# Layer 1's windowed attention in program order on three engines, with its modulation row made in layer 0's FFN

## The chip, the core and the metric

The kernel runs on one core of a Trainium2 chip, as one program. A core has a matrix engine (TensorE, here PE, with its weight loads as PEld), VectorE (DVE), ScalarE (ACT) and GpSimd (POOL), and queues of transfers, most of which SyncE (SP) issues. The engines run side by side; each works through its own list of instructions in order and waits on semaphores for the others. The metric is the device time of one execution in microseconds (us): before, 2740.77 us in the median of three runs (2738.22 to 2741.01).

## What is computed

512 tokens of width 1024 and 256 context rows go through two transformer layers, and the tokens then through a third block. Every normalization is followed by a shift and a scale, and every branch by a gate; these rows come from `silu(c) @ w_mod[l] + b_mod[l]`, six of 1024 per layer. In layer 1 the mixer is windowed attention, in which 16 query heads share 4 key heads of 64:

```
h  = modulate(x, g_pre_mix[1], sh_m, sc_m)
q, k, v = split(h @ wo_in)             # 1024 + 256 + 256 columns; context: k, v alone
q, k = axial_rope(q), axial_rope(k)
one block of 128 queries:              # lax.map over 4 blocks
  s = [q.k(band of 3 blocks, |q-k| <= 128)/8, q.k(256 context)/8, sink[head]]
  p = softmax(s);  o = p[band] @ v + p[ctx] @ v_ctx
y = concat(o) @ wo_out
x = x + gt_m * rmsnorm(y, g_post_mix[1])
h = modulate(x, g_pre_ffn[1], sh_f, sc_f)
x = x + gt_f * rmsnorm(swiglu(h), g_post_ffn[1])
```

Both blocks of queries at an edge have two key blocks in the band, the inner ones three. All is float32; most matrix products are split into a high and a low part (three products for one).

## The kernel before

**Around the change.** Layer 0's FFN (`ffn_pair`, layer 0's tokens and context together) runs eleven iterations over pairs of hidden columns, and ends each with `mod_tick(ticks)`. A tick makes one half of a modulation row: it takes loaded weights of 1 MB each (`w_mod`) and adds them up, scaled per partition, by scalar_tensor_tensor on DVE (line 395). The halves stand in a list of what is to be made (`bg`), of which the FFN may take those it is allowed; what is left is taken by later callers of `mod_tick`, `unit_end` of layer 1's attention among them (two ticks after every second unit). Rows that are made long before their use are stored in DRAM (`parked`) and loaded again where they are used.

**Layer 1** (`layer1`) makes keys and values, then the queries in two halves of 512 columns. `odd_q(1)` makes the second half: matmuls for four token tiles, and behind each tile a rope on DVE and a turn (`stack_q`), which splits the tile into a high part (ACT, line 383) and a low part (DVE, line 386), transposes both on PE (line 407, two rows of x4) and copies them out. The turns go through a list `later`; the last ones are popped one by one while the attention runs.

**The attention** (`attention4`) has 16 units: 2 halves of heads x 4 query blocks x 2, with four heads in each. Units 0, 1, 6 to 9, 14 and 15 have four key tiles (scores 512 wide), the others five (640 wide). It is a generator, one step per key tile:
- `score`: matmuls into a pair of PSUM banks (`pr`, two pairs take turns; line 380, masks line 1436), the reduction to the row maximum (DVE, line 1441), a small operation (398), the exponential with its sum (ACT, line 389). For the second head of a pair: the sink's difference on DVE (392), its exponential on ACT (389, 128x2), an add (392) and a reciprocal (1459) on DVE, and on POOL the scaling of both heads (1462).
- `trans`: four transposes on PE (407) and a copy out on ACT (1469).
- `pv`: the products of a unit with the values (PE, line 1484), then the high part (ACT, 383 into hTh) and the low part (DVE, 386 into hTl) of the result.

Scores run six heads ahead of the transposes. The loop spreads a unit's four scores over its key tiles (with five tiles none before the first), each followed by its `trans`, and calls `pv` of the unit before behind the second. After every score `self.stream.pump(1)` may issue one step of the weight stream: a load, or the split of a loaded weight (ACT line 263, DVE line 264; 1024 wide).

**What sets the order.** A scheduler orders each engine's instructions. Inside `with self.in_order(...)` the engines named keep the order in which the code emits them. For the attention PE alone is named: DVE and ACT are ordered by the scheduler there. Four steps of the generator run before `odd_q(1)`, and the others behind it, each followed by one turn out of `later`.

Of the kernel before, what the change touches and what calls it, by code (L numbers as in the profile page):

```python
# [339 lines left out]
class Core:  # L340
# [1078 lines left out]
    def attention4(self, units, v, odst, unit_end, ahead=6):  # L1419
        nc = self.nc  # L1420

        def score(u, h):
            n, c1, g = u["n"], u["col0"], h // 2
            if h == 0:
                u["sm"], u["nm"] = [self.small(2) for _ in range(2)], [self.small(2) for _ in range(2)]
                u["p"] = []
            sm, nm = u["sm"][g], u["nm"][g]
            sp = self.pair()
            q = u["q"][h]()
            for c0, k, w in u["pieces"][g]:  # L1430
                out = sp.ap[:, c0:c0 + w]
                ms = [m for m in u["mask"] if c0 <= m[0] < c0 + w]
                self.mm(out, q, k(0), start=True)
                self.mm(out, q, k(1), stop=not ms)
                for i, (mc, mi) in enumerate(ms):
                    nc.tensor.matmul(sp.ap[:, mc:mc + P], self.identb, self.maskb[:, mi * P:mi * P + P],
                                     start=False, stop=i == len(ms) - 1, skip_group_check=True)
            s = sp.ap[:, c1:c1 + n]
            i = h % 2
            m = nm[:, i:i + 1]  # L1440
            nc.vector.reduce_max(m, s, axis=AX.X)  # L1441
            if u["sink"] is None:
                self.t1(m, m, u["nscale"][h], ALU.mult)
            else:
                at = u["sink"][g]
                self.ts(m, m, -0.125, self.nsink[:, at + i:at + i + 1], ALU.mult, ALU.min)
            p = self.page()
            self.act(p.ap[:, 0:n], s, AF.Exp, scale=u["scale"][h], bias=m, accum_out=sm[:, i:i + 1])
            sp.done()
            u["p"].append(p)  # L1450
            if i == 0:
                return
            r = self.small(2)
            if u["sink"] is not None:
                es = self.small(2)
                self.tt(es, nm, self.nsink[:, at:at + 2], ALU.subtract)
                self.act(es, es, AF.Exp)
                self.tt(sm, sm, es, ALU.add)
            nc.vector.reciprocal(r, sm)
            for i in range(2):  # L1460
                p = u["p"][2 * g + i].ap[:, 0:n]
                nc.gpsimd.tensor_scalar(p, p, r[:, i:i + 1], 0.0, op0=ALU.mult, op1=ALU.add)  # L1462

        def trans(u, kt):
            b = self.bank()
            for h in range(4):
                self.tr(b.ap[:, P * h:P * h + P], u["p"][h].ap[:, kt * P:kt * P + P])
            pt = self.slot()
            nc.scalar.copy(pt.ap, b.ap)  # L1469
            b.done()  # L1470
            if kt == len(u["kt"]) - 1:
                for p in u["p"]:
                    p.done()
            return pt

        def pv(u, pts):

            ob = self.bank()
            last = len(pts) - 1
            for kt, pt in enumerate(pts):  # L1480
                vv = v(u["kt"][kt], u["kvs"])
                for g in range(2):
                    r = 64 * g
                    nc.tensor.matmul(ob.ap[r:r + 64, 0:256], vv[:, r:r + 64], pt.ap[:, 256 * g:256 * g + 256],  # L1484
                                     start=kt == 0, stop=kt == last, skip_group_check=True)
                pt.done()
            src = ob.ap[:, 0:256].rearrange("p (k n) -> p k n", k=2)
            dh, dl = odst(u, 0), odst(u, 1)
            self.hi(dh, src)
            self.lo(dl, src, dh)  # L1490
            ob.done()
            unit_end(u)

        self.psum.layout(True)
        waiting = deque((u, h) for u in units for h in range(4))
        for _ in range(ahead):
            score(*waiting.popleft())
            yield
        prev = None
        for u in units:  # L1500
            n, pts = len(u["kt"]), []
            for kt in range(n):
                for _ in range(4 * (kt + 1) // n - 4 * kt // n):
                    if waiting:
                        score(*waiting.popleft())
                        self.stream.pump(1)
                pts.append(trans(u, kt))
                yield
                if kt == 1 and prev:
                    pv(*prev)  # L1510
            prev = u, pts
        pv(*prev)
        self.psum.layout(False)
        yield

# [157 lines left out]
    def ffn_pair(self, win, wout, l, vecs, mid, ticks):  # L1673
# [56 lines left out]
        for j in range(11):  # L1730
            eg = st.need(("fm", win, l, 0, 8, 256 * j))
            eu = st.need(("fm", win, l, 0, 8, HID + 256 * j))
            at = [(eg, 0), (eg, 1), (eu, 0), (eu, 1)]
            bx, bc = [], []
            if j == 0:
                subs = [st.get(*a) for a in at]
                bx = [self.bank() for _ in range(4)]
                for h in range(2):
                    for i, s in enumerate(subs):
                        self.fm(bx[i].ap[:, H * h:H * h + H], s, 0, acts, range(8), H * h, H)  # L1740
                        if h == 1 and mid and i == 1:
                            mid.popleft()()
                while mid:
                    mid.popleft()()
            for i in range(4):
                if i % 2 == 0:
                    bc.append(self.bank())
                s = subs[i] if j == 0 else st.get(*at[i])
                if j:
                    bx.append(self.bank())  # L1750
                    self.fm(bx[i].ap, s, 0, acts, range(8), 0, TOK)
                self.fm(bc[i // 2].ap[:, CTX * (i % 2):CTX * (i % 2) + CTX], s, 0, acts, range(8), TOK, CTX)
                s.done()
            if j == 10:
                strict = self.in_order(mybir.EngineType.Activation, mybir.EngineType.DVE)
                strict.__enter__()
            hx.append(self.page())
            if j % 2 == 0:
                hc.append(self.page())
            for i in range(2):  # L1760
                g = self.slot()
                self.act(g.ap, bx[i].ap, AF.Silu)
                self.tt(hx[j].ap[:, TOK * i:TOK * i + TOK], g.ap, bx[2 + i].ap, ALU.mult)
                bx[i].done()
                bx[2 + i].done()
                g.done()
            g, o = self.slot(), 512 * (j % 2)
            self.act(g.ap, bc[0].ap, AF.Silu)
            self.tt(hc[j // 2].ap[:, o:o + 512], g.ap, bc[1].ap, ALU.mult)
            for b in bc + [g]:  # L1770
                b.done()
            self.mod_tick(ticks)
            if j == 9:
                hidden.prep(0)
                hidden.prep(1)
# [16 lines left out]
    def layer1(self):  # L1792
# [6 lines left out]
        later = deque(self.carry)  # L1799
# [68 lines left out]
        def odst(u, i):  # L1868
            a = 4 * u["kvs"] + 2 * u["hp"]
            return self.hT[i][:, a:a + 2, u["o"] * P:u["o"] * P + P]  # L1870

        def unit_end(u):
            if u["hp"] == 1:
                qT.pop((u["o"], u["kvs"])).done()
                self.mod_tick(2)
        attn = self.attention4(units, v, odst, unit_end)
        for _ in range(4):
            next(attn)
        later = self.odd_q(1)
        self.rope_b.done()  # L1880
        with self.in_order(mybir.EngineType.PE):
            for _ in attn:
                if later:
                    later.popleft()()
        for b in kT + kcp + [V, Vc]:
            b.done()
# [498 lines left out]
```

## Time and profile before

| | before |
|---|---|
| median of 3 runs | 2740.77 us |
| lowest, highest | 2738.22, 2741.01 us |
| the profiled execution | 2742.69 us |
| its span in the trace | 2740.9 us |
| granted PE clock, mean | 0.991 |
| PE busy | 2654.6 us, 97% |
| DVE busy | 1527.7 us, 56% |
| ACT busy | 1038.7 us, 38% |
| POOL busy | 271.0 us, 10% |

The span runs from the first instruction to the last; 1.8 us of the execution lie around it. Busy time is summed over instructions; PE's clock is granted at one of two levels, of which 1.00 is the higher and 0.50 the lower. A wait is written behind the instruction that waited: `[2.67 <-DVE pg L386]` says that the engine sat idle for 2.67 us until an instruction of line 386 on DVE was done. Lines 380 to 407 are helpers, one line for an operation wherever it is called, so rows are told apart by their tiles. Layer 0's FFN fills roughly 440 to 740 us of the span, layer 1's attention 1030 to 1176.

### The profile page before, as it was taken

The page shows a single profiled execution, that of the slowest core. Times are in us where ns is not written, and L with a number is a line of the kernel's source. Part 1 is how long each engine was busy: PE and PEld are TensorE (multiplying, and loading weights), DVE is VectorE, ACT ScalarE, POOL GpSimd, SP SyncE. Part 2 cuts the span into 40 slices and gives each one's busy share as a digit, 9 for nine tenths or more (in the row PEclk, how much of TensorE's full clock was granted, in tenths as well). Part 3 has the DMA queues.
Part 4 walks back from the last instruction along what each step waited for, and adds up shares of the span by engine and source line. Part 5 has one row for each costly group of instructions (what it writes and reads, how often), then busy time and mean ns, then how long its engine had stood idle before and what let it go on. Part 6 is the DMA issues. An engine that isn't in the chain of part 4 may idle for free.

```text
span 2740.9 us, 33578 instructions
## 1 busy us (share of the span) xinstructions
PE 2654.6 (97%) x13396; PEld 2207.6 (81%) x13396; DVE 1527.7 (56%) x2427; ACT 1038.7 (38%) x1844; POOL 271.0 (10%) x331
## 2 busy tenths in 40 slices
PE   6978999999999998999999999999999999999998
PEld 5767888888888786688888888888888788888887
DVE  6789596544364756657653286233567475642242
ACT  4446442112144446743223233223445643322231
POOL 3633110000000102310000000000002320000000
PEclk9999999999999998999999999999999999999999
DMA  7123344333244122027663246323222133452220
GB/s 243 51 70 106 129 146 162 124 130 131 77 139 138 50 70 62 24 81 233 216 200 108 81 161 226 116 100 124 85 92 70 54 123 119 142 169 93 100 93 31
DMA packets 212270, 320.16 MB, mean 117 GB/s; under 512 B 10072, under 2 KB 137816, under 8 KB 212112
## 3 DMA queue, kind: packets, MB, share of 16 engines
q1 hardware_dynamic: 207584, 316.35, 34.8%
q8 instruction: 105, 1.72, 0.3%
q10 hardware_dynamic: 4528, 1.65, 0.3%
q14 instruction: 53, 0.43, 0.1%
HBM read 310.56 MB, written 7.41 MB: 116 GB/s over the span
## 4 chain that ended last, share of the span: by engine, by line
PE 54%; DVE 3%; ACT 1%; POOL 1%; issue 1%; DMA 0%; POOLq 0%; DVEq 0%; ACTq 0%
PE bk L380 51%; DVE pg L395 1%; PE bk L407 1%; PE bk L1484 1%; DVE pg L392 1%; ACT pg L389 1%; PE pr L380 1%; POOL smalls L404 0%; DVE pg L264 0%; PE bk L2097 0%; ACT pg L1469 0%; DVE smalls L1441 0%; DVE pg L386 0%; POOL pg L1462 0%; DMA pg<-in_rel_dram 0%
## 5 line engine op out<-in xcount | busy, mean ns | idle before, releaser
L380 PE MATMUL bk<-hTh,pg 128*128 128x512 f32 (+1 forms) x3776 | 1118.7, 376 | 0.0
L380 PEld LDWEIGHTS bk<-hTh,pg 128*128 128x128 f32 x3776 | 693.4, 188 | 125.9 <-ACT hTh L383 0.2
L380 PE MATMUL bk<-pg,pg 128*128 128x512 f32 (+1 forms) x3902 | 775.4, 355 | 2.9 <-ACT pg L383 2.4
L380 PEld LDWEIGHTS bk<-pg,pg 128*128 128x128 f32 x3902 | 653.8, 189 | 108.8 <-ACT pg L383 2.7
L380 PE MATMUL bk<-hTl,pg 128*128 128x512 f32 (+1 forms) x1888 | 708.9, 376 | 1.0 <-DVE hTl L386 1.0
L264 DVE TENSOR_TENSOR pg<-raw,pg 128x1024 fp32r<-128x1024 f32 x365 | 437.9, 1228 | 206.7 <-ACT pg L263 152.8
L263 ACT CAST pg<-raw 128x1024 fp32r<-128x1024 f32 x366 | 371.9, 1048 | 270.5 <-DMA raw<-in_w_ffn_in_dram 91.3
L380 PEld LDWEIGHTS bk<-hTl,pg 128*128 128x128 f32 x1888 | 356.0, 189 | 62.8 <-DVE hTl L386 1.4
L392 DVE TENSOR_TENSOR pg<-pg,bk 128x512 f32<-128x512 f32 x107 | 73.1, 686 | 427.0 <-PE bk L380 401.0
L380 PE MATMUL bk<-pg,hTh 128*128 128x512 f32 (+1 forms) x976 | 295.7, 389 | 2.8 <-ACT hTh L383 2.5
L395 DVE SCALAR_TENSOR_TENSOR pg<-raw,cols,pg 128x512 f32<-128x512 f32 x350 | 260.8, 769 | 17.6 <-DMA raw<-in_w_ada_dram 11.5
L389 ACT ACTIVATE pg<-bk 128x512 f32<-128x512 f32 x115 | 67.7, 596 | 521.4 <-PE bk L380 369.2
L404 POOL TENSOR_TENSOR smalls<-smalls,mhalf 128x1 f32<-128x1 f32 (+1 forms) x67 | 44.3, 661 | 1940.0 <-DVE smalls L395 1938.5
L383 ACT CAST pg<-pg 128x512 fp32r<-128x512 f32 (+2 forms) x231 | 131.6, 589 | 228.9 <-PE bk L380 131.2
L380 PEld LDWEIGHTS bk<-pg,hTh 128*128 128x128 f32 x976 | 181.0, 191 | 38.0 <-ACT hTh L383 3.0
L407 PE MATMUL bk<-ident,pg 128*128 128x128 f32 x1048 | 166.0, 285 | 44.9 <-DMA pg<-in_w_mod_dram 11.3
L380 PE MATMUL bk<-pg,hTl 128*128 128x512 f32 (+1 forms) x488 | 183.6, 387 | 0.4 <-DVE hTl L805 0.4
L407 PEld LDWEIGHTS bk<-ident,pg 128*128 128x128 f32 x1048 | 124.5, 145 | 73.6 <-DVE pg L395 15.9
L386 DVE TENSOR_TENSOR pg<-pg,pg 128x512 fp32r<-128x512 f32 (+1 forms) x207 | 127.3, 628 | 95.8 <-ACT pg L383 95.3
L392 DVE TENSOR_TENSOR pg<-bk,pg 128x512 f32<-128x512 f32 (+2 forms) x100 | 56.3, 598 | 156.8 <-ACT junk L389 99.3
L380 PE MATMUL pr<-pg,pg 128*128 128x256 f32 (+2 forms) x416 | 105.4, 363 | 19.3 <-ACT pg L389 16.5
L380 PEld LDWEIGHTS bk<-pg,hTl 128*128 128x128 f32 x488 | 92.8, 190 | 18.9 <-DVE hTl L805 1.1
(131 smaller groups left out, 1789.1 us busy)
## 6 DMA issues: line engine op xcount, KB each, us to landing
raw<-in_w_ffn_in_dram SPq DMA_DIRECT2D x44, 1024.0 KB
raw<-in_ffn_w_gu_dram SPq DMA_DIRECT2D x44, 1024.0 KB
raw<-in_w_mod_dram SPq DMA_DIRECT2D x40, 1024.0 KB
raw<-in_w_ada_dram SPq DMA_DIRECT2D x36, 1024.0 KB
raw<-in_ffn_w_down_dram SPq DMA_DIRECT2D x22, 1024.0 KB
raw<-in_w_in_dram SPq DMA_DIRECT2D x22, 1024.0 KB
raw<-in_w_ffn_out_dram SPq DMA_DIRECT2D x21, 1024.0 KB
pg<-parked SPq DMA_DIRECT2D x18, 512.0 KB
```

Source lines behind the costliest of these rows:

```text
L263: nc.scalar.copy(R(o[0]), src)
L264: self.lower.tensor_tensor(R(o[1]), src, o[0], op=ALU.subtract)
L380: self.nc.tensor.matmul(out, R(a), R(b), start=start, stop=stop, skip_group_check=True)
L383: self.nc.scalar.copy(R(out), src)
L386: self.nc.vector.tensor_tensor(R(out), src, hi, op=ALU.subtract)
L389: self.nc.scalar.activation(out=out, in_=src, func=func, **k)
L392: (eng or self.nc.vector).tensor_tensor(out, a, b, op=op)
L395: self.nc.vector.scalar_tensor_tensor(out, a, s, b, op0=op0, op1=op1)
L404: self.nc.gpsimd.tensor_tensor(out, v, self.mhalf[:, :n], op=ALU.pow)
L407: self.nc.tensor.transpose(out, src, self.ident)
L1484: nc.tensor.matmul(ob.ap[r:r + 64, 0:256], vv[:, r:r + 64], pt.ap[:, 256 * g:256 * g + 256], start=kt == 0, stop=kt == last, skip_group_ch ...
```

## The change

Five edits:
1. `pv` no longer evacuates its result. It returns a closure `evac`, which holds the high and low part, the release of the bank, `unit_end` and one `pump(1)`; the loop calls it behind the next step's `trans`.
2. `pump(1)` after every score is gone: the one in `evac` remains, once a unit.
3. Layer 0's FFN ticks `ticks + j % 2` times in iteration j: 27 instead of 22 over the eleven iterations. The four halves that it takes in addition make the tokens' gate row of layer 1's FFN (`x, 1, gt_f`); that row is now parked and loaded once more.
4. Six steps instead of four run before `odd_q(1)`.
5. The attention keeps the code's order on PE, ACT and DVE, and the left-over turns are popped only from the fifth step behind `odd_q(1)` on.

```diff
@@ attention4: end of pv @@
-            src = ob.ap[:, 0:256].rearrange("p (k n) -> p k n", k=2)
-            dh, dl = odst(u, 0), odst(u, 1)
-            self.hi(dh, src)
-            self.lo(dl, src, dh)
-            ob.done()
-            unit_end(u)
+
+            def evac():
+                src = ob.ap[:, 0:256].rearrange("p (k n) -> p k n", k=2)
+                dh, dl = odst(u, 0), odst(u, 1)
+                self.hi(dh, src)
+                self.lo(dl, src, dh)
+                ob.done()
+                unit_end(u)
+                self.stream.pump(1)
+
+            return evac
...
-        prev = None
+        prev = evac = None
         for u in units:
             n, pts = len(u["kt"]), []
             for kt in range(n):
                 for _ in range(4 * (kt + 1) // n - 4 * kt // n):
                     if waiting:
                         score(*waiting.popleft())
-                        self.stream.pump(1)
                 pts.append(trans(u, kt))
+                if evac:
+                    evac()
+                    evac = None
                 yield
                 if kt == 1 and prev:
-                    pv(*prev)
+                    evac = pv(*prev)
             prev = u, pts
-        pv(*prev)
+        pv(*prev)()
@@ ffn_pair @@
-            self.mod_tick(ticks)
+            self.mod_tick(ticks + j % 2)
@@ layer1 @@
-        for _ in range(4):
+        for _ in range(6):
             next(attn)
         later = self.odd_q(1)
         self.rope_b.done()
-        with self.in_order(mybir.EngineType.PE):
-            for _ in attn:
-                if later:
+        with self.in_order(mybir.EngineType.PE, mybir.EngineType.Activation, mybir.EngineType.DVE):
+            for i, _ in enumerate(attn):
+                if later and i > 3:
                     later.popleft()()
```

Three places show the new order. The first is PE where the projection of `odd_q(1)` ends. In the kernel before, the turns of token tile 2 (`pg_7820`) and tile 3 (`pg_7868`) stand there in a row, and the scores (`pr`) come after them:

```order
L380 MATMUL bk_74<-pg_7702,hTh 128x512
L380 MATMUL bk_74<-pg_7701,hTl 128x512
L407 MATMUL bk_76<-ident,pg_7820 128x128 x4
L407 MATMUL bk_73<-ident,pg_7820 128x128 x4
L407 MATMUL bk_75<-ident,pg_7868 128x128 x4
L407 MATMUL bk_74<-ident,pg_7868 128x128 x4
L380 MATMUL pr_7652<-pg_7351,pg_7183 128x256 x2
```

In the changed kernel only tile 2's turn (`pg_7871`) stands at that place, and behind it come the first transposes of unit 0 (`pg_7694` and three more pages of exponentials):

```order
L380 MATMUL bk_76<-pg_7760,hTh 128x512
L380 MATMUL bk_76<-pg_7759,hTl 128x512
L407 MATMUL bk_74<-ident,pg_7871 128x128 x4
L407 MATMUL bk_73<-ident,pg_7871 128x128 x4
L407 MATMUL bk_75<-ident,pg_7694 128x128
L407 MATMUL bk_75<-ident,pg_7703 128x128
L407 MATMUL bk_75<-ident,pg_7718 128x128
L407 MATMUL bk_75<-ident,pg_7727 128x128
L380 MATMUL pr_7685<-pg_7391,pg_7223 128x256 x2
```

Tile 3's turn has moved some forty rows down, behind the first transposes of unit 1. The second place is ACT at the same point. Before, the exponential into `pg_7890` stands ahead of the two copies of tile 3's turn into `pg_7867`:

```order
L383 CAST pg_7868<-pg_7712 128x8x64
L383 CAST pg_7819<-bk_76 128x512
L383 CAST pg_7819<-bk_73 128x512
L389 ACTIVATE pg_7890,smalls<-pr_7651,smalls 128x512
L383 CAST pg_7867<-bk_75 128x512
L383 CAST pg_7867<-bk_74 128x512
```

After, the high part of tile 3 (`pg_7924`) and tile 2's copies (`pg_7870`) stand ahead of the seventh and eighth exponentials (`pg_7946`, `pg_7960`), and the first copy of unit 0 between these:

```order
L263 CAST pg_7902<-raw_59 128x1024
L263 CAST pg_7912<-raw_59 128x1024
L383 CAST pg_7924<-pg_7918 128x8x64
L383 CAST pg_7870<-bk_74 128x512
L383 CAST pg_7870<-bk_73 128x512
L389 ACTIVATE pg_7946,smalls<-pr_7686,smalls 128x512
L1469 COPY pg_6455<-bk_75 128x512
L389 ACTIVATE pg_7960,smalls<-pr_7685,smalls 128x512
```

The two weight splits (line 263) have come ahead of all of these. The third place is DVE in the steady part. Before, a unit's reductions (line 1441) are mixed by the scheduler with the add (392, 128x2 from `smalls` alone) and the reciprocal of the pair of heads before:

```order
L386 TENSOR_TENSOR hTl<-bk_74,hTh 128x2x128
L1441 TENSOR_REDUCE smalls<-pr_7652 128x1
L398 TENSOR_SCALAR smalls<-smalls,nsink 128x1
L392 TENSOR_TENSOR smalls<-smalls,nsink 128x2
L1441 TENSOR_REDUCE smalls<-pr_7651 128x1
L398 TENSOR_SCALAR smalls<-smalls,nsink 128x1
L392 TENSOR_TENSOR smalls<-smalls 128x2
L1459 RECIPROCAL smalls<-smalls 128x2
```

After, with five key tiles:

```order
L1441 TENSOR_REDUCE smalls<-pr_7685 128x1
L398 TENSOR_SCALAR smalls<-smalls,nsink 128x1
L392 TENSOR_TENSOR smalls<-smalls,nsink 128x2
L392 TENSOR_TENSOR smalls<-smalls 128x2
L1459 RECIPROCAL smalls<-smalls 128x2
L386 TENSOR_TENSOR hTl<-bk_73,hTh 128x2x128
L1441 TENSOR_REDUCE smalls<-pr_7686 128x1
L398 TENSOR_SCALAR smalls<-smalls,nsink 128x1
```

The next reduction has moved from ahead of the add to behind the add, the reciprocal and the low part (line 386 into `hTl`).

## Rows read from the trace of the kernel before

**Rows 1.** Windows: us, busy time and (xcount) of each engine, PEclk, DMA share, GB/s.

```profile
440.00:490.00 50.00, 49.89 (x285) 43.55 (x285) 29.38 (x39) 12.10 (x16) 0.00 (x0) 1.00 0.44 150
1030.00:1180.00 150.00, 133.28 (x953) 99.59 (x953) 94.19 (x248) 103.38 (x252) 45.46 (x60) 0.94 0.15 42
```

**Rows 2.** Timeline (start us, us, instruction, idle before), behind the second queries' projection.

```profile
1031.87 1.03 PE L407 MATMUL bk<-ident,pg 128*128 128x128 f32 x8
1035.58 1.97 PE L407 MATMUL bk<-ident,pg 128*128 128x128 f32 x8 [2.67 <-DVE pg L386]
...
1034.70 1.06 ACT L383 CAST pg<-bk 128x512 fp32r<-128x512 f32 x2
```

**Rows 3.** Windows again, columns as in the first group, three stretches for the clock.

```profile
132.00:136.00 4.00, 1.59 (x13) 1.27 (x11) 4.00 (x8) 1.82 (x4) 3.76 (x6) 1.00 0.00 0
1036.00:1044.00 8.00, 6.64 (x32) 5.96 (x30) 5.55 (x12) 3.66 (x10) 0.00 (x0) 0.50 0.09 28
1076.00:1090.00 14.00, 11.58 (x87) 8.40 (x85) 9.30 (x27) 10.65 (x26) 4.72 (x6) 1.00 0.01 2
```

**Rows 4.** Timeline, DVE and PE at the stall near 1065 us.

```profile
1060.83 1.23 DVE L264 TENSOR_TENSOR pg<-raw,pg 128x1024 fp32r<-128x1024 f32 x1 [1.95 <-ACT pg L263]
...
1065.00 0.62 PE L380 MATMUL pr<-pg,pg 128*128 128x384 f32 x2 [2.46 <-ACT pg L389]
```

**Rows 5.** PE's waits from 1080 to 1176: in total, times, longest.

```profile
PE pr L380 <- ACT pg L389: 4.9, 11, 0.7
```

**Rows 6.** Timeline, five-tile units: PE, then ACT, then DVE.

```profile
1057.99 1.30 PE L1484 MATMUL bk<-pg,pg 128*64 128x256 f32 x10
...
1144.24 0.62 PE L380 MATMUL pr<-pg,pg 128*128 128x384 f32 x2 [0.43 <-ACT pg L389]
...
1146.65 0.60 PE L380 MATMUL pr<-pg,pg 128*128 128x384 f32 x2
...
1148.04 2.38 PE L1484 MATMUL bk<-pg,pg 128*64 128x256 f32 x20
...
1166.04 1.30 PE L1484 MATMUL bk<-pg,pg 128*64 128x256 f32 x10
...
1143.31 0.79 ACT L389 ACTIVATE pg<-pr,smalls 128x640 f32<-128x640 f32 x1
...
1146.49 0.79 ACT L389 ACTIVATE pg<-pr,smalls 128x640 f32<-128x640 f32 x1
...
1147.36 0.57 ACT L1469 COPY pg<-bk 128x512 f32<-128x512 f32 x1
...
1142.20 0.82 DVE L1441 TENSOR_REDUCE smalls<-pr 128x1 f32<-128x640 f32 x1
...
1143.41 0.82 DVE L1441 TENSOR_REDUCE smalls<-pr 128x1 f32<-128x640 f32 x1
...
1144.40 0.15 DVE L392 TENSOR_TENSOR smalls<-smalls 128x2 f32<-128x2 f32 x1
```

**Rows 7.** Timeline, copy, high part, low part and reduction in one row (ACT, then DVE).

```profile
1131.29 0.58 ACT L1469 COPY pg<-bk 128x512 f32<-128x512 f32 x1
1131.75 0.39 ACT L383 CAST hTh<-bk 128x256 fp32r<-128x256 f32 x1
...
1132.17 0.42 DVE L386 TENSOR_TENSOR hTl<-bk,hTh 128x256 fp32r<-128x256 f32 x1 [1.69 <-ACT hTh L383]
1132.55 0.82 DVE L1441 TENSOR_REDUCE smalls<-pr 128x1 f32<-128x640 f32 x1
```

**Rows 8.** Timeline, a four-tile unit (ACT, then DVE).

```profile
1095.44 0.69 ACT L389 ACTIVATE pg<-pr,smalls 128x512 f32<-128x512 f32 x1
...
1098.21 0.69 ACT L389 ACTIVATE pg<-pr,smalls 128x512 f32<-128x512 f32 x1
...
1094.41 0.69 DVE L1441 TENSOR_REDUCE smalls<-pr 128x1 f32<-128x512 f32 x1
...
1099.16 0.15 DVE L392 TENSOR_TENSOR smalls<-smalls 128x2 f32<-128x2 f32 x1
```

## The prediction

> **What bounds the kernel now.** I read the stretches first, since they say where TensorE (PE) has anything to give. In layer 0's FFN the row for 440 to 490 us shows PE busy 49.89 of 50 us beside 29.38 us of VectorE (DVE): what other engines do there shows in the time only if it makes PE wait [rows 1]. Layer 1's attention is the other kind: from 1030 to 1180 us PE is busy 133.28 of 150 us, so 16.7 us are idle [rows 1], at three sorts of place. (a) The ramp. The second queries' projection ends at 1031.87, which I call X; the turn (transposes) of token tile 2 follows at once, and the turn of tile 3 comes at 1035.58 after 2.67 us idle: PE runs in program order, and tile 3's rope and split are not ready [rows 2]. The granted clock of the 8 us from 1036 is 0.50, the lower of its two levels (1.2 of 2.4 GHz) [rows 3]. (b) A stall of 2.46 us before the score at 1065.00: it waits for an exponential, that for a reduction, and the reduction for a weight split at 1060.83, which had itself held DVE for 1.95 us of waiting for ScalarE (ACT) [rows 4]. (c) In the steady part, 1080 to 1176, scores wait for exponentials 11 times, 4.9 us in all [rows 5]: the loop through DVE and ACT runs close to PE's own work.
>
> So the prize is near 16.7 us plus what the half clock costs, and a new order on ACT and DVE touches the very loop of (c). It decides, so it is priced first.
>
> **The steady cycle, five key tiles.** Call R2 the reduction at 1142.20, that of the second score behind a PV. Before, its exponential E2 starts 1.11 later (1143.31). The next reduction R3 does not wait for E2: the scheduler put it at 1143.41, 1.21 behind R2 and ahead of the sink's add (1144.40), which needs E2 and the small exponential after it. PE's next unit starts with its score S1' at 1146.65, R2 + 4.45, and PV follows that by 1.39 (1148.04) [rows 6].
> After, DVE and ACT keep the order of the code: on DVE R2, the sink's add and reciprocal, the low part of the deferred evacuation, and only then R3; on ACT E2, the sink exponential, the copy C2 of the turned tile, and then the high part, for which the low part waits. Each link has a row. From an exponential over the sink exponential to the copy: 0.87 (1146.49 to 1147.36) [rows 6]. From the copy to the high part 0.46 (1131.29 to 1131.75), to the low part 0.42 (1132.17), to the reduction 0.38 (1132.55) [rows 7]. So R3 starts at R2 + 1.11 + 0.87 + 0.46 + 0.42 + 0.38 = R2 + 3.24, where it was 1.21. E3 follows 1.11 later, at 4.35. S1' goes into the pair of PSUM banks that E3 reads, and a score starts 0.93 behind the start of such an exponential (1143.31 to 1144.24) [rows 6]: S1' at R2 + 5.28 instead of 4.45, **+0.83 us a cycle**, the two scores and the PV behind it staying as they are. A cycle of 9.2 us becomes one of 10.05.
>
> **The cycle with four key tiles** (units 0, 1, 6 to 9, 14, 15 of 16). The rows are 512 wide there. Reduction to exponential takes 1.03 (1094.41 to 1095.44), an exponential 0.69, and from the second exponential of a pair of heads (1098.21) to the sink's add it is 0.95 (1099.16); with the add and the reciprocal, 0.32 by their durations, 1.27 to a next reduction that stands behind them [rows 8]. The high and low parts stand behind the third copy, between the third and the fourth reduction. Once around: 1.03 + 0.69 + 0.46 + 0.42 + 0.38 = 2.98 from R3 to R4; 1.03 + 1.27 to the next unit's R1 (5.28); 1.03 + 0.69, the copy behind that exponential (0.55, an estimate from the step of two copies in [rows 2]) and 1.27 to R3 again: **8.82 us**. It is one chain: PE waits for it, whatever PE has to do in the cycle.
>
> From PV of unit 1 (1057.99) to PV of unit 13 (1166.04) are 12 cycles and 108.05 us [rows 6]. Mine are 10, 10, 9.85, 9.2, 8.8, 8.8, 9.5, 9.5, 10, 10, 9.85, 9.2 (the 9.2, 9.5 and 9.85 where units of both widths meet are estimates between 8.8 and 10): 114.7, that is **+6.65**. This already holds the end of stall (b), since the weight splits now run ahead of the loop: 2.46 and a clock loss of some 0.6 (an estimate) are gone.
>
> **The ramp.** Six scores instead of four are issued ahead of the second queries' projection, in which PE has no gap: two scores, some 1.35 us of PE, come before X and are gone behind it, which is nothing in sum. Behind X tile 3's turn no longer holds PE; turn of tile 2, transposes of unit 0, a score and transposes fill it till X + 2.4. Then the next score needs the seventh exponential, and in ACT's code order that stands behind the high part of tile 3's queries and two evacuation copies; the high part needs the last rope add, and that in DVE's code order stands behind the eighth score's reduction, at X + 2.2. Reduction and add of 0.69 each take it to 3.6, the high part to 4.2, the two copies (1.06 [rows 2]) to 5.26, the exponential to 5.95, the score to 6.1. PE idles 3.7 us there in place of 2.67. I take it that the clock falls again, since after 2.67 us it did [rows 2, 3]; but from 132 to 136 us PE was busy 1.59 of 4 us, and the clock stayed at 1.00 [rows 3]. The Trainium skill (TensorE: Matmul & The Clock Gate, Part 1: The HAM clock gate) calls the half rate the default, which activity releases. By that alone each such gap costs the clock, and the row of 132 us shows one that did not. With the fall PV of unit 0 comes at X + 16.2, without at 12.7, so 3.5 us stay in the range. The PV of unit 1 has to await the copy of its fourth tile and ends as if it had begun at X + 23.5, where it was X + 26.12 [rows 2, 6]; with X 1.35 later that is **-1.3 us**. At the end the last unit's evacuation has no score left to hide behind: +0.5 (0 to 1, an estimate from [rows 7]).
>
> **The modulation moved to layer 0's FFN.** Five more ticks in eleven iterations take four halves out of layer 1: 16 scalar_tensor_tensor on DVE, four loads of 1 MB on SP's queue, one store and one reload of the parked row. Even at the 1.23 us of the split [rows 4] that is under 20 us of DVE over several stretches with 20 us free in each 50 [rows 1], and PE waits for none of it. What stands behind it is on SP's queue, the weights of the next iteration. Cost taken: 0 (bounds: -0.5 for what DVE is spared in attention, and +10 if weights come 2 us late in each of the five longer iterations).
>
> **The sum**: 6.65 - 1.3 + 0.5 + 0 = +5.85 us on the profiled execution of 2742.69 (span 2740.9 and 1.8 around it). That one stands 1.9 above the median, 2740.77; on the median the forecast is 2746.6.
>
> **Rivals.** (A) The loop of DVE and ACT doesn't bind: ACT is busy 103.38 and DVE 94.19 of the 150 us [rows 1], so if copies and high parts come early enough, the cycles stay at 108.05 less stall (b), 3.1, and the ramp keeps its gain: -3.1 - 1.3 + 0.5 = -3.9, or -7.4 where the clock also stays up behind X: 2733.4 to 2736.9. It turns on whether R3 starts under 2 us behind R2. For it: 4.9 us of waits in 96 are few [rows 5]. Against: R3 ran ahead of the add (1143.41, 1144.40) [rows 6], and code order forbids just that. (B) My loop holds, but the clock stays up behind X: +2.35, 2743.1. (C) Waiting more, PE loses its clock again and again. A cycle holds some 8 us of PE work (108.05 x 133.28 / 150 / 12), 16 at half clock against 9.6, so 6.4 for each cycle that loses it; with two to five of them, 2759 to 2779. The page's rule allows this; against it, from 1076 to 1090 us PE was busy 11.58 of 14 and the clock 1.00 [rows 3]. (D) The moved loads make layer 0's weights late: 2750 to 2757.
>
> **How the numbers follow.** A measurement of this kernel tells 0.2%, 5.5 us, from no change: 2735.3 to 2746.3. Chances: my sum 0.42, of which 0.12 end a little lower, inside that band; (B) 0.18, inside; (A) 0.24, of which 0.18 below 2735.3; (C) 0.08; (D) 0.08. Faster 0.18, same 0.36, slower 0.46. The range runs from below A to D's upper end, 2732 to 2757.
>
> **What would show it.** Right: the reduction behind a sink's add never ahead of it, and over 3 us behind the one before where an evacuation stands between; PV starts 10 and 8.8 us apart; PE's waits for exponentials some three times 4.9 us; no stall as at 1065; a gap of 3 to 4 us a little behind X, with clock 0.50 after it; layer 0's FFN as long as before. Wrong: cycles of 9 and 7 us (A), a clock under 1.00 behind the ramp (C), PE waits in layer 0 (D).

## The result: 2781.8 us, slower by 1.46%

| | before | after |
|---|---|---|
| median | 2740.89 us (4 runs) | 2781.81 us (4 runs) |
| lowest, highest | 2738.22, 2742.79 us | 2778.24, 2782.42 us |
| span of the profiled execution | 2740.9 us | 2780.6 us |
| PE busy | 2654.6 us | 2672.6 us |

The ratio is 1.0146, with a 95% interval of 1.0134 to 1.0158. The forecast was 2746.6 with a range to 2757: the direction was right, the size far too small, 5.85 us against some 40. Of the 39.7 us between the two profiled executions, PE is busy for 18.0 us longer, with as many rows (13396), and idle for 21.7 us longer.

Four instants cut the 39.7 us into pieces: the turn of tile 2 behind the second queries' projection (X), PV of unit 1, PV of unit 13, and the end. These are PE's rows of the changed kernel (start us, us, instruction, idle before it); before, X was 1031.87 [rows 2], and the two PVs were 1057.99 and 1166.04 [rows 6].

```profile
1057.45 1.47 PE L407 MATMUL bk<-ident,pg 128*128 128x128 f32 x12
...
1063.27 0.62 PE L380 MATMUL pr<-pg,pg 128*128 128x384 f32 x2 [2.93 <-ACT pg L389]
...
1077.51 1.52 PE L1484 MATMUL bk<-pg,pg 128*64 128x256 f32 x12
...
1205.36 1.95 PE L1484 MATMUL bk<-pg,pg 128*64 128x256 f32 x16
```

| from, to | before | after | difference |
|---|---|---|---|
| start to X | 1031.87 | 1057.45 | +25.58 |
| X to PV of unit 1 | 26.12 | 20.06 | -6.06 |
| PV of unit 1 to PV of unit 13 | 108.05 | 127.85 | +19.80 |
| PV of unit 13 to the end | 1574.86 | 1575.24 | +0.38 |

**Up to X.** The windows from 400 to 800 us (us, busy time and (xcount) of PE, PEld, DVE, ACT, POOL, then PEclk, DMA share, GB/s), layer 0's FFN, first of the kernel before:

```profile
400.00:800.00 400.00, 399.89 (x2244) 349.70 (x2243) 205.16 (x277) 98.06 (x143) 0.00 (x0) 1.00 0.40 132
```

and of the changed one:

```profile
400.00:800.00 400.00, 388.72 (x2148) 336.74 (x2147) 208.82 (x282) 90.92 (x133) 0.00 (x0) 0.97 0.42 139
```

PE, which had no gap there, is now idle for 11.28 us, and its clock is down for a part of the time; DVE has hardly more to do than before (208.82 against 205.16 in this stretch). PE's waits from 400 to 1000 us, of which the kernel before has only the last line (1.4 in 3):

```profile
PE bk L380 <- DVE pg L386: 3.7, 4, 1.4
PE bk L380 <- ACT pg L263: 2.8, 2, 1.6
PE bk L380 <- DVE pg L264: 2.6, 3, 1.3
PE bk L380 <- ACT pg L383: 2.2, 2, 1.2
PE bk L407 <- DVE pg L395: 1.3, 3, 0.9
```

Apart from that line, half is for splits of weights (lines 263 and 264), half for the two parts (383, 386) of a finished modulation row, for which PE has to wait where it has no products of the next weights to do in between. Splits of weights come late. These are ACT's splits (line 263) between 410 and 448 us before:

```profile
416.85 2.00 ACT L263 CAST pg<-raw 128x1024 fp32r<-128x1024 f32 x2 [10.76 <-DMA raw<-in_w_ffn_in_dram]
422.66 2.00 ACT L263 CAST pg<-raw 128x1024 fp32r<-128x1024 f32 x2 [3.81 <-DMA raw<-in_w_ffn_in_dram]
441.58 3.89 ACT L263 CAST pg<-raw 128x1024 fp32r<-128x1024 f32 x4
```

and the only ones in the same stretch after, with two other rows of ACT ahead of them:

```profile
432.54 0.60 ACT L389 ACTIVATE pg<-bk 128x512 f32<-128x512 f32 x1 [16.32 <-DVE pg L392]
440.88 0.60 ACT L389 ACTIVATE pg<-bk 128x512 f32<-128x512 f32 x1 [7.74 <-DVE pg L392]
...
442.92 3.88 ACT L263 CAST pg<-raw 128x1024 fp32r<-128x1024 f32 x4
```

Four splits that used to lie in the middle of an iteration have gone to its end, where PE needs them at once. Neither ACT's time nor the data lacked: ACT is idle for 16.32 and 7.74 us before, and no transfer runs from 428 to 443 us, so the loads had landed.

**In the loop.** PE's waits from 1057 to 1217 us of the changed kernel (in total, times, longest) answer to [rows 5], which had 4.9 us in 11 from 1080 us on (8.5 in 14 from 1057 on, with the stall of [rows 4]):

```profile
PE pr L380 <- ACT pg L389: 23.3, 24, 2.9
PE bk L407 <- POOL pg L1462: 2.8, 7, 0.4
PE bk L1484 <- ACT pg L1469: 2.3, 3, 0.8
```

DVE and ACT in a cycle with five key tiles, answering to [rows 6 and 7]:

```profile
1103.04 0.79 ACT L389 ACTIVATE pg<-pr,smalls 128x640 f32<-128x640 f32 x1 [1.84 <-DVE smalls L398]
...
1103.92 0.57 ACT L1469 COPY pg<-bk 128x512 f32<-128x512 f32 x1
1104.38 0.38 ACT L383 CAST hTh<-bk 128x256 fp32r<-128x256 f32 x1
...
1101.87 0.82 DVE L1441 TENSOR_REDUCE smalls<-pr 128x1 f32<-128x640 f32 x1 [2.13 <-PE pr L380]
...
1104.80 0.42 DVE L386 TENSOR_TENSOR hTl<-bk,hTh 128x256 fp32r<-128x256 f32 x1 [0.39 <-ACT hTh L383]
1105.14 0.68 DVE L1441 TENSOR_REDUCE smalls<-pr 128x1 f32<-128x512 f32 x1
```

R3 starts at 1105.14, 3.27 us behind R2 (1101.87): exponential at +1.17, copy 0.88 later, high part 0.46, low part 0.42, reduction 0.34 (this R3 is the first of a unit with four key tiles, 512 wide). The forecast had 3.24, by the same links. What it did not have is in the windows of the same loop, where the clock falls in one stretch after the other:

```profile
1110.00:1115.00 5.00, 4.20 (x33) 3.17 (x29) 2.29 (x8) 2.41 (x8) 1.19 (x3) 1.00 0.00 0
1115.00:1120.00 5.00, 3.64 (x18) 3.35 (x18) 2.77 (x10) 3.58 (x10) 1.67 (x3) 0.66 0.00 0
...
1130.00:1135.00 5.00, 5.00 (x32) 3.33 (x28) 1.61 (x6) 2.21 (x8) 1.43 (x3) 0.68 0.00 0
1140.00:1145.00 5.00, 5.00 (x29) 2.93 (x26) 1.75 (x6) 2.40 (x7) 1.85 (x3) 0.66 0.00 0
```

These are all the waits of PE from 1077 to 1206 us that are longer than 0.9 us:

```profile
1116.36 0.80 PE L380 MATMUL pr<-pg,pg 128*128 128x256 f32 x2 [1.72 <-ACT pg L389]
...
1128.10 0.51 PE L380 MATMUL pr<-pg,pg 128*128 128x256 f32 x2 [1.62 <-ACT pg L389]
...
1138.54 0.50 PE L380 MATMUL pr<-pg,pg 128*128 128x256 f32 x2 [1.62 <-ACT pg L389]
...
1149.67 0.62 PE L380 MATMUL pr<-pg,pg 128*128 128x384 f32 x2 [1.72 <-ACT pg L389]
...
1180.71 0.83 PE L380 MATMUL pr<-pg,pg 128*128 128x384 f32 x2 [2.72 <-ACT pg L389]
...
1201.62 0.80 PE L380 MATMUL pr<-pg,pg 128*128 128x256 f32 x2 [1.74 <-ACT pg L389]
```

The clock falls six times in the loop, each time about the end of one of these six waits or within 2 us behind it. The longest, 2.72 us, has a cause of its own: the one weight split that is left in the loop stands on DVE between the low part and R3 (1177.26), and R3 comes 5.27 us behind R2 (1173.33 to 1178.60).

### The profile page after: what moved, and what is told of

Same layout as the page of the kernel before. It is cut to its first block, busy times and chain, and to the rows that moved or that the text cites. A ratio compares the mean times of both kernels' runs of the same rounds, so it can differ in the third digit from the quotient of the medians.

```text
span 2780.6 us, 33550 instructions
## 1 busy us (share of the span) xinstructions
PE 2672.6 (96%) x13396; PEld 2215.9 (80%) x13396; DVE 1526.3 (55%) x2427; ACT 1035.3 (37%) x1844; POOL 270.3 (10%) x331
## 4 chain that ended last, share of the span: by engine, by line
PE 55%; DVE 6%; ACT 2%; issue 1%; POOL 1%; DMA 1%; DVEq 0%; ACTq 0%; POOLq 0%
PE bk L380 51%; DVE pg L395 2%; DVE pg L392 1%; PE bk L407 1%; PE bk L1484 1%; PE pr L380 1%; ACT pg L389 1%; DVE pg L264 1%; POOL smalls L404 1%; DVE smalls L1441 1%; DMA raw<-in_w_ada_dram 0%; DMA raw<-in_w_ffn_in_dram 0%; ACT pg L1469 0%; PE bk L2104 0%; DVE hTl L386 0%
## 5 line engine op out<-in xcount | busy, mean ns | idle before, releaser
L380 PEld LDWEIGHTS pr<-pg,pg 128*128 128x128 f32 x416 | 71.0, 201 | 54.9 <-ACT pg L389 40.3
```

Of the source, the lines that this page charges most:

```text
L380: self.nc.tensor.matmul(out, R(a), R(b), start=start, stop=stop, skip_group_check=True)
```

## The experiments

Two questions stood: what makes layer 0's FFN lose 22 us, and which part of the order makes the loop lose 20. Each kernel ran beside the kernel before on the same chip, whose median there was 2740.1 to 2740.5. The loop is the time from PV of unit 1 to PV of unit 13 in the run's trace, so it is one execution: the changed kernel and e1, whose loops have the same order, are 3.2 us apart (127.85 and 124.68), and e2, e7 and e11, also of one order, 0.25. e3 and e4 have two executions each. In the kernels with added lines at the top, line numbers are one higher.

| run | median, us | ratio and 95% interval | loop, us |
|---|---|---|---|
| e1_gain_queue | 2781.64 | 1.0147 [1.0130, 1.0164] | 124.68 |
| e2_pe_order | 2756.56 | 1.0053 [1.0038, 1.0068] | 101.47 |
| e3_pe_dve_order | 2763.66 | 1.0081 [1.0056, 1.0105] | 106.93 |
| e4_pe_act_order | 2757.65 | 1.0059 [1.0039, 1.0079] | 102.45 |
| e5_no_ticks | 2779.24 | 1.0143 [1.0127, 1.0158] | 146.63 |
| e6_no_ticks_pe | 2745.94 | 1.0021 [1.0012, 1.0030] | 113.28 |
| e7_three_mods_pe | 2739.69 | 1.0001 [0.9992, 1.0010] | 101.72 |
| e8_six_late | 2737.91 | 0.9990 [0.9982, 0.9999] | 104.84 |
| e9_turns_twice | 2784.11 | 1.0159 [1.0145, 1.0173] | 123.77 |
| e10_evacuate_now | 2766.52 | 1.0095 [1.0081, 1.0109] | 110.03 |
| e11_late_ticks_pe | 2737.37 | 0.9991 [0.9982, 0.9999] | 101.71 |
| e12_no_deferral_pe | 2740.99 | 1.0005 [0.9996, 1.0014] | 104.34 |

### Layer 0's FFN: is it the queue?

SyncE's queue had a suspect. Its waits from 395 to 470 us of the changed kernel have this line, a small load that waits for a page, with weight loads behind it:

```profile
SPq L462 <- DVE pg L392: 20.8, 1, 20.8
```

The edit of e1 sends that load by another queue:

```diff
-        self.nc.sync.dma_start(gb.ap, src[o:o + 512].partition_broadcast(P))
+        self.gain_queue.dma_start(gb.ap, src[o:o + 512].partition_broadcast(P))   # gpsimd in ffn_pair
```

> The changed kernel, but in layer 0's FFN the small load of a gain row (2 KB, line 462), which waits for a page, is issued from GpSimd's queue instead of SyncE's. Theory (the queue): the 24 us lost in layer 0's FFN come from SyncE's queue, where that load waits 20.8 us for a page and the weight loads stand behind it. Then FFN's PE waits go and the time falls by 20 to 25 us, to 2757 to 2762. Rival (volume: five more ticks are too much for DVE or for the transfers): the time stays within 4 us of 2781.8, and PE waits for weight splits as before.

Measured: 2781.64. The theory of the queue fell. The same stretch of e1:

```profile
400.00:800.00 400.00, 387.20 (x2158) 335.94 (x2157) 208.50 (x282) 90.95 (x134) 3.76 (x7) 0.99 0.42 139
```

PE is idle as long as before the edit (12.8 us), and ACT's first splits after 415 us are still four together, at 443.99. The page was a consequence, not the cause.

The second look was at what decides where a split stands in the code. Loads and splits come from one stream, in which an iteration's modulation halves stand ahead of the next iteration's weights. `pump`, called as each piece of weights is used up, goes along that stream, but runs one step of modulation per call; `mod_tick` at the iteration's end forces the rest. With two halves an iteration, eight steps, the pump gets past them in time to split weights in the middle; with three, twelve steps, it doesn't, and the splits are emitted behind the tick. In the trace they also run late. It is not the code's order that holds them there: `ffn_pair` sets ACT and DVE to it only in the last of its eleven iterations, and why the scheduler, which orders the others, leaves the splits behind is not shown. The edit of e7 (on top of the order of e2, below):

```diff
-        mods = 1
+        mods = self.mods        # 3 in ffn_pair's eleven iterations, 1 elsewhere
...
-        with self.in_order(mybir.EngineType.PE, mybir.EngineType.Activation, mybir.EngineType.DVE):
+        with self.in_order(mybir.EngineType.PE):
```

> The changed kernel with the code's order on PE alone (as e2_pe_order, but all small loads on SyncE's queue), and in layer 0's FFN one call of the pump may run three steps of modulation instead of one. Theory (the one step a call holds the next iteration's weight splits in the code behind all halves of an iteration; with twelve steps instead of eight it never gets past them): weight splits come earlier, the PE waits in layer 0's FFN fall to a third, 2733 to 2742. Rival (the volume on DVE and the transfers): as e2, 2753 to 2759.

Measured: 2739.69, 16.9 below e2, which differs from it by the pump and by the queue of e1 (which had moved nothing). Its window of the FFN:

```profile
400.00:800.00 400.00, 398.24 (x2234) 347.89 (x2234) 220.51 (x297) 99.82 (x146) 0.00 (x0) 1.00 0.43 144
```

and ACT's first splits behind 410 us in it:

```profile
419.17 2.00 ACT L264 CAST pg<-raw 128x1024 fp32r<-128x1024 f32 x2 [0.57 <-DMA raw<-in_w_ffn_in_dram]
427.06 2.00 ACT L264 CAST pg<-raw 128x1024 fp32r<-128x1024 f32 x2 [5.90 <-DMA raw<-in_w_ffn_in_dram]
```

The splits are back in the middle of the iteration, PE's idle time falls from 11.3 to 1.8 us, and the clock is at 1.00. So the pump's limit is shown to be the cause of the late splits and of nearly all of the loss (X is at 1037.24, for 1056.35 in e2). The volume was never the matter: DVE is busier here (220.51) than in the changed kernel.

### The loop: which engine's order?

The edits of e2, e3 and e4 are the engines named (all on top of e1):

```diff
-        with self.in_order(mybir.EngineType.PE, mybir.EngineType.Activation, mybir.EngineType.DVE):
+        with self.in_order(mybir.EngineType.PE):                              # e2
+        with self.in_order(mybir.EngineType.PE, mybir.EngineType.DVE):        # e3
+        with self.in_order(mybir.EngineType.PE, mybir.EngineType.Activation): # e4
```

> As e1_gain_queue, but the attention keeps the code's order on PE alone; DVE and ACT are ordered by the scheduler again. Theory (code order on DVE and ACT makes the loop): cycles go back to 9.1 and 7.1 us, the clock stays up in the loop, the ramp keeps its 6 us: 2731 to 2738, faster than the kernel before. Rival (the deferred evacuation or the pump once a unit makes the loop long): within 5 us of e1.

> As e1_gain_queue, with the code's order on PE and DVE, ACT free. Theory (the reduction held behind add and low part is DVE's order): most of the loop's loss stays, 2750 to 2760; the next reduction starts about 3 us behind the one before where an evacuation stands between. Rival (ACT's order is what costs): near e2.

> As e1_gain_queue, with the code's order on PE and ACT, DVE free. Theory (DVE's order): reductions are hoisted ahead of the add again, most of the loss goes: 2732 to 2742. Rival (ACT's order): near e1, 2755 to 2760.

The totals of these three hold FFN's loss, which e1 had not removed, so they can't be held against the times expected; the loops tell them apart. With PE's order alone 101.47 us, 6.6 less than before the change; with DVE's order added 106.93; with ACT's 102.45; with both (e1) 124.68. The theory that DVE's order is the cost fell, and so did the rival, ACT's: alone they cost 5.5 and 1.0 us, and both together 23.2, of which 15.2 are idle time of PE and 8.0 its slower clock (busy 100.56 for 92.59). DVE of e4, where DVE is free, and of e3, where ACT is, show why (e4, then e3):

```profile
1143.90 0.83 DVE L1442 TENSOR_REDUCE smalls<-pr 128x1 f32<-128x640 f32 x1 [2.13 <-PE pr L381]
...
1145.17 0.82 DVE L1442 TENSOR_REDUCE smalls<-pr 128x1 f32<-128x640 f32 x1
```

```profile
1105.13 0.37 ACT L384 CAST hTh<-bk 128x256 fp32r<-128x256 f32 x1 [0.33 <-PE bk L1485]
...
1105.92 0.69 DVE L1442 TENSOR_REDUCE smalls<-pr 128x1 f32<-128x512 f32 x1 [2.02 <-PE pr L381]
...
1108.40 0.68 DVE L1442 TENSOR_REDUCE smalls<-pr 128x1 f32<-128x512 f32 x1
```

In e4 R3 is hoisted, 1.27 us behind R2, as before the change. In e3 it stands behind add and low part, but ACT, free, ran the high part before the exponential (1105.13), so the low part waits for nothing and R3 comes after 2.48 us (2.1 of e3's 5.5 us lie in one cycle of 11.36 us, where the weight split stands on DVE ahead of R3 as well). Only with both orders does the low part wait for exponential, copy and high part one after the other.

### The deferred evacuation

```diff
-                    evac = pv(*prev)
+                    pv(*prev)()          # e10, on the changed kernel
```

> The changed kernel with the evacuation right behind PV again, in the code's order on all three engines. Theory (R3 is late because the low part stands between add and R3): the high part now stands ahead of the second exponential behind PV and the low part ahead of R2, while PE is at the score; R3 follows R2 by some 2.5 us in place of 3.27 (1.11 + 1.08 + 0.32), a five-tile cycle takes 9.3 to 9.5, the 12 cycles 113 to 120: 2767 to 2775. Rival (the deferral helps, as the code's author may have meant: ACT would wait for PV): 2781 or more.

Measured: 2766.52, 15 us below the changed kernel, half a microsecond under what was expected; the loop is 110.03, shorter than the 113 to 120 of the theory, though two of its cycles (11.97 and 11.45 us) hold a weight split and a fall of the clock. R2 and R3 in it:

```profile
1092.90 0.82 DVE L1441 TENSOR_REDUCE smalls<-pr 128x1 f32<-128x640 f32 x1
...
1095.28 0.17 DVE L1459 RECIPROCAL smalls<-smalls 128x2 f32<-128x2 f32 x1
1095.36 0.80 DVE L1441 TENSOR_REDUCE smalls<-pr 128x1 f32<-128x640 f32 x1
```

R3 follows R2 by 2.46 us, where 2.51 was worked out: the add and the reciprocal still stand ahead of it, the low part no longer does. So under the code's order the deferral is the larger part of the loop's loss. Where the scheduler orders ACT and DVE it is the other way, if anything. The edit of e12 takes the deferral away from e7 (`pv` evacuates and pumps once at its end).

> As e7_three_mods_pe, without the deferred evacuation: PE alone in the code's order, evacuation and one pump right behind PV. It tells what the deferral is worth where the scheduler orders ACT and DVE. Theory (nothing: the scheduler puts high and low part where they fit): within 2 us of e7. Rival (the deferral of PE's order against the bank's release shortens the loop): 3 us or more slower than e7.

Measured: 2740.99 against 2739.69, 1.3 us apart with overlapping intervals, so within the 2 us of the theory, though the traces' loops (104.34 and 101.72) differ by more, since e12's holds a cycle of 11.12 us with a weight split.

### The clock

The forecast for the loop was 114.7, the measurement 127.85. The windows of the loop itself, after, and in e2, where the clock stays up:

```profile
1077.51:1205.36 127.85, 103.81 (x715) 74.95 (x714) 64.23 (x190) 74.85 (x196) 36.97 (x50) 0.92 0.00 1
```

```profile
1076.06:1177.53 101.47, 92.59 (x715) 68.76 (x714) 64.84 (x187) 76.29 (x192) 36.23 (x49) 1.00 0.01 1
```

The same 715 rows take PE 92.59 us at full clock and 103.81 here: 11.2 us are the clock's. PE's idle time is 24.0 us. The forecast's 114.7 less 92.6 of work is 22.1 us idle: in sum the waits were forecast to 2 us, and the rest of the miss is the clock. That the clock's time adds to the loop and does not fill waits is borne out by e1, which has the same order: PE is busy for 3.25 us less there (100.56), idle as long (24.1), and the loop is 3.17 us shorter. To see whether PE's idleness costs the clock, e9 gives PE work that nobody needs:

```diff
             for h in range(4):
                 self.tr(b.ap[:, P * h:P * h + P], u["p"][h].ap[:, kt * P:kt * P + P])
+            for h in range(4):
+                self.tr(b.ap[:, P * h:P * h + P], u["p"][h].ap[:, kt * P:kt * P + P])
```

> The changed kernel, but in the attention every set of four transposes of exponentials is done twice into the same bank: 0.44 us more of PE's work 72 times, some 32 us that the result doesn't need. Theory (13 of the 20 us that the loop lost are PE's clock, which falls because PE waits): with PE busier the clock stays at 1.00 in the loop, and the 12 cycles from PV of unit 1 to PV of unit 13 take no more than 127.85 + 3, in spite of 12 x 2 us more work; the whole within 4 us of 2781. Rival (the clock is a consequence of no weight, the cycles are a chain): the added transposes stand in the chain about twice a cycle, 0.9 us, and the 12 cycles take 138 or more, the whole 2790 or more.

Measured: 2784.11, within the theory's 4 us of the changed kernel, and the loop:

```profile
1076.32:1200.09 123.77, 114.20 (x940) 92.86 (x939) 63.57 (x188) 73.61 (x195) 37.02 (x50) 1.00 0.00 1
```

PE does 225 more rows of work, and the loop is no longer (123.77, where the changed kernel has 127.85 and e1 124.68): the clock is at 1.00 all along, PE busy 114.20 of 123.77. The scores that waited for 1.62 to 1.74 us wait for 1.01 to 1.19 here, and the one behind the weight split for 2.29. The median is no better, so this is no repair, but it shows that the clock stays up where PE is busier and waits less: the falls come of PE's waiting. Not each wait brings one: in e1 two of 1.62 and 1.61 us (before 1129.04 and 1137.84) had no fall behind them. Whether the length of a wait or the idle share around it decides is not shown.

### The ramp and the modulation alone

e8 is the kernel before with two of the edits, six scores ahead and the turns from the fifth step on:

```diff
-        for _ in range(4):
+        for _ in range(6):
             next(attn)
...
-            for _ in attn:
-                if later:
+            for i, _ in enumerate(attn):
+                if later and i > 3:
```

> The kernel before with two edits alone: six scores ahead of the second queries, and the left-over turns from the fifth step on. Theory (the ramp gains 6 us by itself): 2732 to 2737. Rival (the gain is given back, since the pump after every score puts more weight splits into the loop): 2739 to 2743.

Measured: 2737.91, ratio 0.9990 [0.9982, 0.9999]: a gain, of some 2 us in the medians. In the trace X is at 1035.39, 3.5 us later than before (two scores, 1.35, waits for weight splits of 1.2, and 0.8 by which this execution is behind at 330 us already), PV of unit 1 at 1055.20, and the loop takes 104.84 with the clock at 1.00.

e5 and e6 leave the modulation where it was: the changed kernel with the old ticks, and the same with PE's order alone (the weight stream is held one page earlier there, so that the pages suffice for the rest).

```diff
-            self.mod_tick(ticks + j % 2)
+            self.mod_tick(ticks)
...
+        st.reserve = 8                   # during the attention, 7 before and after
```

> The changed kernel with layer 0's FFN ticking as before (22 ticks), so the gate row's four halves stay in layer 1's attention; the weight stream is held one page earlier there, so that the pages suffice. Theory (the five ticks cost 24 us in layer 0's FFN, whatever queue their small loads take; the attention costs 16 on its own): 2754 to 2761. Rival (in code order the halves in the attention cost what the FFN gains): 2770 or more.

> As e5_no_ticks, but the code's order on PE alone. Theory: what is left of the change (six scores ahead, late turns, deferred evacuation, one pump a unit) gains some 8 us by ramp and stall: 2730 to 2736, faster than the kernel before. Rival (the scheduler mixes the halves into the loop of DVE as before): 2738 to 2744.

Measured: 2779.24, as the rival had it, and 2745.94, which is slower than even the rival's 2738 to 2744. Layer 0's FFN is whole again in both, but the halves are back in the attention: the loop takes 146.63 in e5, with one cycle of 22.8 us, and 113.28 in e6. Under the code's order they stand on DVE between the low part and the next reduction (e5):

```profile
1090.27 0.42 DVE L386 TENSOR_TENSOR hTl<-bk,hTh 128x256 fp32r<-128x256 f32 x1 [0.39 <-ACT hTh L383]
1090.61 1.98 DVE L395 SCALAR_TENSOR_TENSOR pg<-raw,cols,pg 128x512 f32<-128x512 f32 x2
...
1094.68 3.10 DVE L395 SCALAR_TENSOR_TENSOR pg<-raw,cols,pg 128x512 f32<-128x512 f32 x4
```

In the same cycle DVE also waits for 3.65 us for a weight split (1101.44), whose data ACT had awaited. So moving the halves was worth its while for the attention (127.85 for 146.63), and lost in the FFN by the pump's limit what it gained.

Last, a version from what was learned, e11: e7 with the five added ticks in the last five iterations.

```diff
-            self.mod_tick(ticks + j % 2)
+            self.mod_tick(ticks + (j > 5))
```

> As e7_three_mods_pe, but the five added ticks lie in the last five of the eleven iterations (one in each), where DVE is least busy. Theory: the 1.7 us of PE waits that e7 keeps at the first boundary go, the rest stays: 2734 to 2739, faster than the kernel before by 1 to 6 us. Rival (the last iterations have no room: the rows of the other block are flushed there): 2740 to 2750.

Measured: 2737.37, ratio 0.9991 [0.9982, 0.9999], some 44 us below the changed kernel and 2.7 below the kernel before; PE's waits in the FFN's iterations fall from 1.7 to 0.6 us. It and e8 beat both kernels, by an amount near the limit of what is to be measured.

## Why the prediction was wrong

- **The modulation in layer 0's FFN** is the step that failed: "Cost taken: 0", with bounds of -0.5 and +10. It cost 22 us (X at 1057.45 against 1035.39 in e8, which has the same scores ahead of X). From 400 us to X, PE's 3347 rows are busy for 632.18 us in e8, beside 3.21 idle, and for 643.67 here, beside 13.78 idle: 10.6 us are waits, and 11.5 go with the clock, whose mean is 0.98 there and 1.00 in e8. The argument went by DVE's free time and by SyncE's queue. Both were the wrong resource: e1 emptied the queue of its suspect and changed nothing, and e7 did the added work with X at 1037.24, under 2 us behind e8. What the step overlooked is that a tick also moves what is emitted behind it: the weight splits, by the pump's one step a call. Rival (D) had the outcome, with another cause and half the size.
- **The clock in the loop**, rival (C) at 0.08. The forecast took it for an alternative to its own chain, when it is what the chain leads to: 11.2 us. Evidence against it was one stretch of 14 us with PE busy 83% at full clock [rows 3]; that share said nothing of single waits, which were at most 0.7 us in the loop before [rows 5] and are 1.62 to 2.72 us at the six falls after. The Trainium skill (TensorE: Matmul & The Clock Gate, A second HAM failure mode: psum-queue depth-cycling) says that short idle times between groups of matmuls can make the clock go back and forth; the windows of 1115, 1130 and 1140 us agree (0.66 to 0.68), and in e9, with less idleness, the clock stays at 1.00.
- **The chain** was right link by link: R3 at R2 + 3.27 for 3.24; 24.0 us of idle time for 22.1. It also held in e10 (2.46 for 2.51). Of its twelve cycles, by the PV starts of the trace, five ran at full clock: 10.81, 10.16, 9.77, 9.27 and 10.79 us, for 10, 10, 9.85, 8.8 and 10. Of the others some were mis-sized apart from the clock: 13.15 (12.16 at full clock in e1) for 10, where the forecast had all weight splits ahead of the loop and one was left in it; 11.82 and 11.88 for 9.2, where five tiles give way to four, with PE busy for 1.3 us longer than at full clock; and 7.36 for 9.5. That these nearly cancel in the sum is luck. The forecast had called the chain the code's order on DVE and ACT, and e3 and e4 show that it needs both. Rival (A) is out.
- **The ramp** went rival (B)'s way in this execution: PE waited 2.93 us at 1063.27, less than the 3.7 worked out, and the clock from 1060 to 1068 is 1.00. PV of unit 0 came at 1071.03, X + 13.6, for 12.7 without the fall and 16.2 with it. In e1, with the same order, the clock fell behind the same wait (2.95 us, 0.79 from 1060 to 1068), as the forecast had it; PV of unit 0 came at X + 14.4 and PV of unit 1 at X + 20.9, for 20.1 without the fall. So whether the clock falls there differs between executions, and the difference is 0.8 us and not 3.5. X itself came later by 3.5 us in e8 and not by the two scores' 1.35, in part for weight splits: the projection is not quite without gaps.
- **The sum.** 22.1 for 0 in the FFN, 19.8 for 6.65 in the loop, -2.5 for -1.3 in the ramp (3.5 - 6.06), 0.4 for 0.5 at the end. (B), (C) and (D) were weighed as alternatives, each with its own time; all three came true at once, beside the forecast's own chain, and the range ended at (D)'s upper end instead of reaching their sum.

What stays open: what the loop would take were the clock at 1.00 without e9's added transposes, since these stand in the chain too (127.85 less 11.2, 116.6, is an estimate from the busy times above); and why the scheduler leaves the late weight splits late.

## What to carry to other kernels

Before an engine is put into the code's order, follow one loop through all engines so ordered: here the order of one cost 5.5 or 1.0 us, and that of both, which couples their waits, 23. Where code emits work from a stream with limits, an added call can cost what it pushes back, not what it does: look where the next weights' preparation stands after the change. And causes that make PE wait are not alternatives: add them up, with the clock as their common consequence.

## What the runs showed of the hardware

A wait of 2.93 us did not cost PE its clock (1060 to 1068 us: PE busy 4.17 of 8 us, 1.00), where one of 2.67 us did [rows 2, 3], and the same wait of e1, 2.95 us, did too (0.79). In the loop each of six falls came with a wait of 1.62 to 2.72 us, and the stretches whose waits were all under 0.9 us (1077 to 1114, 1155 to 1178) had none. Added work on PE kept its clock up, so that a loop with 225 more rows took no longer (e9: 123.77 us, for 127.85 and 124.68).
